# Depthwise convolution of 31 taps: four taps of a channel tile on ScalarE and GpSimd in place of TensorE

## The chip, the cores and the metric

One core of a Trainium2 chip runs the whole program in one launch. The metric is the time of that launch on the device, in microseconds, as the median of several runs; a profile of one execution stands beside it.

## The reference

Two transformer blocks run one after the other on 512 latent tokens (width 1024), the first with 256 context tokens beside them. The first block has a conformer convolution, a feed-forward with a convolution of width 3, a window attention and a second such feed-forward; the second block has an attention, a recurrent mixer, a memory attention and a third feed-forward. All is fp32. The change touches the conformer convolution alone, which runs near the start, for the latent and the context tokens:

```python
def dwconv(x, w, b):
    k = w.shape[0]                      # 31
    pad = (k - 1) // 2
    y = lax.conv_general_dilated(x, w[:, None, :], window_strides=(1,), padding=[(pad, pad)],
                                 dimension_numbers=('NWC', 'WIO', 'NWC'), feature_group_count=x.shape[-1])
    return y + b

def conformer_conv(h, w_pw1, b_pw1, w_dw, b_dw, ln_g, ln_b, w_pw2, b_pw2):
    u = h @ w_pw1 + b_pw1               # 1024 -> 2048
    a, g = jnp.split(u, 2, axis=-1)
    v = a * jax.nn.sigmoid(g)
    v = dwconv(v, w_dw, b_dw)           # each channel by itself, 31 taps along the tokens
    v = jax.nn.silu(layernorm(v, ln_g, ln_b))
    return v @ w_pw2 + b_pw2
```

## The kernel before

Channels lie on the 128 partitions and tokens along the free dimension, so a width of 1024 is eight channel tiles (`KT`). Every matrix product of the two blocks is made of three matmuls over high and low parts (`mm3`, L155 to L165): a weight half of 128x1024 is cast to its high part on ScalarE (`wh`, L143), and VectorE subtracts that from the raw weight for the low part (`wl`, L144). The raw weights come by DMA on SP's queue.

The convolution's stage is a loop over `j`, the channel tiles. `pw1(j)` does the first matrix product for tile `j` into five PSUM banks taken in turn; ScalarE takes the sigmoid of the gate, and VectorE writes the gated product `v` (L542 for the context, L543 for the latent tokens) into one of two buffers `vb`. A tile of `v` is 832 columns: 512 latent and 256 context tokens with zeros for the padding between and around them, so that one instruction over 798 columns (`AW`) does one tap for both.

The 31 taps of a tile are shared out by `NPE`. The first 4 x `NPE[j]` are TensorE's. For these `pw1(j)` writes `v` to DRAM (`vd`) and reads it back four times, with each group of 32 channels laid out four times at shifts of 0 to 3 columns (`S`). `diagonals(j)` makes 32x32 diagonal blocks of the tap weights on VectorE (`dg`, L571), and `dwconv(j)` multiplies (L583): one matmul does four taps of 32 channels, four of them make 128 channels, `NPE[j]` of those follow each other into one PSUM tile, for the latent and for the context part. The remaining taps are `taps(j)`: VectorE multiplies a shifted `v` by one weight per channel and adds it to `accp` (L560). The first of them is a product alone, on ScalarE for tiles 0 and 1 (L562), and from tile 2 on it adds `negc`, an offset taken from tile 0 (L564). `accp` and `prod` have two buffers each. At the end of `dwconv(j)` VectorE evicts: PSUM plus bias plus `accp` into `y` (L585).

The code issues for each `j`: `pw1(j)`, `taps(j)`, one or two pieces of a modulation product (`ada_pe`, L370, with raw weights of its own), the sums of squares of tile `j` - 2 (`sums`, L605 to L613, ScalarE writes the square into `prod`), and then `diagonals(j - 1)` and `dwconv(j - 1)`. The last tile is split into its latent and context part so that the layer norm can start early. The order on each engine is not that of the code: a planner orders the instructions by priority and by its own costs before the launch, puts in the semaphores, and from then on each engine's queue is fixed and in order. A buffer is taken again when its last reader is done.

GpSimd does nothing in this stage but a few fills of constants at its start.

Of the kernel before, what the change touches and what calls it, by code (L numbers as in the profile page):

```python
# [11 lines left out]
AF = mybir.ActivationFunctionType  # L12
ALU = mybir.AluOpType
# [4 lines left out]
KT = D // 128  # L18
SEQ = 512
CTX = 256  # L20
TOK = SEQ + CTX
# [30 lines left out]
def build(tc, ins, out, stop=None, dbg=None):  # L52
    ctx = ExitStack()
    with ctx:
        _build(ctx, tc, ins, out, stop, dbg)


def _build(ctx, tc, ins, out, stop, dbg):
    nc = tc.nc
    pe, act, dve, pool, sp = nc.tensor, nc.scalar, nc.vector, nc.gpsimd, nc.sync  # L60
# [32 lines left out]
    def ps(cols=512, tag="mm", parts=128):  # L93
        n = cur.turn.get(tag, 0)
        cur.turn[tag] = n + 1
        p, bufs = cur.tags[tag][n % len(cur.tags[tag])]
        return p.tile([parts, cols], F32, tag=tag, bufs=bufs, name=tag)

    def wk(cols, tag, bufs=1, dt=F32, parts=128, first=False):

        p, bufs = cur.sm, cur.bufs.get(tag, bufs)
        if cur.st and tag in ("cv", "u"):
            n = cur.turn.get(tag, 0)
            cur.turn[tag] = n + 1
            p, bufs = (cur.st, 2) if first or n % bufs < 2 else (p, bufs - 2)
        return p.tile([parts, cols], dt, tag=tag, bufs=bufs, name=tag)
# [15 lines left out]
    def V(name, i=0, n=1):  # L122
        o, c = _VOFF[name]
        assert i + n <= c
        return vec[:, o + i : o + i + n]
# [304 lines left out]
    SW = C0 + CTX + 16  # L430
    AW = C0 + CTX
    FILL = (0, 2, 2, 2, 2, 1, 1, 1, 1)
    NPE = (4, 4, 4, 4, 4, 4, 4, 5)
    ORD = (8, 'x', 9, 10, 'q', 11)
    LAT, CT = slice(0, SEQ), slice(SEQ, TOK)
    cur.raw, cur.w = 3, 3
# [4 lines left out]
    with sub("a_x", "xp"), sub("a_w", "wp"), sub("a_s", "sm"):  # L441
# [11 lines left out]
        R = wk(TOK, "sg")  # L453
        S = None
        for k in range(KT):
            q = wk(TOK, "prod", 2)
            for t, s in zip(h[k], (LAT, CT)):
                act.activation(out=q[:, s], in_=t, func=AF.Square)
            if S is None:
                S = q  # L460
            else:
                S2 = wk(AW, "accp", 2)[:, 0:TOK]
                dve.tensor_tensor(out=S2, in0=S, in1=q, op=ALU.add)
                S = S2
# [44 lines left out]
        dwt = wk(512, "dwt")  # L509
# [41 lines left out]

        def taps(j):

            acc = wk(AW, "accp", 2)
            v = vb[j % 2]
            for a, b in ((0, AW),) if j < KT - 1 else ((0, SEQ), (C0, AW)):
                for t in range(4 * NPE[j], 31):
                    w, x = dwt[:, 256 + 32 * j + t : 257 + 32 * j + t], v[:, t + a : t + b]
                    if t > 4 * NPE[j]:
                        dve.scalar_tensor_tensor(out=acc[:, a:b], in0=x, scalar=w, in1=acc[:, a:b], op0=ALU.mult, op1=ALU.add)  # L560
                    elif j < 2:
                        act.activation(out=acc[:, a:b], in_=x, func=AF.Copy, scale=w)  # L562
                    else:
                        dve.scalar_tensor_tensor(out=acc[:, a:b], in0=x, scalar=w, in1=negc[:, a:b], op0=ALU.mult, op1=ALU.add)  # L564
            parts[j] = acc

        def diagonals(j):

            n = NPE[j]
            dg = wk(640, "dg", 1)[:, 0 : n * 128]  # L570
# [5 lines left out]
        def dwconv(j, dg, which=(0, 1)):  # L576
            n, S, acc = NPE[j], shifts[j], parts[j]
            pieces = [(ps((512, 256)[q]), (0, C0)[q], (512, 256)[q], (LAT, CT)[q]) for q in which]
            for m in range(n):
                for p, o, w, _ in pieces:  # L580
                    for g in range(4):
                        c = 32 * (n * g + m)
                        pe.matmul(p[32 * g : 32 * g + 32], dg[:, c : c + 32], S[g][:, 4 * m + o : 4 * m + o + w], start=m == 0, stop=m == n - 1, tile_position=(0, 32 * g))  # L583
            for p, o, w, s in pieces:
                dve.scalar_tensor_tensor(out=y[j][:, s], in0=p, scalar=V("b_dw", j), in1=acc[:, o : o + w], op0=ALU.add, op1=ALU.add)  # L585
            if j == 0:
                offset()
            elif j == 1:
                add_offset(y[1])
# [14 lines left out]

        def sums(j, which=(0, 1), sq=None):  # L605

            sq = sq or wk(TOK, "prod", 2)
            s = slice((LAT, CT)[which[0]].start, (LAT, CT)[which[-1]].stop)
            act.activation(out=sq[:, s], in_=y[j][:, s], func=AF.Square)
            for i in which:  # L610
                s = (LAT, CT)[i]
                for q, x in ((2 * i, y[j][:, s]), (2 * i + 1, sq[:, s])):
                    pe.matmul(SS[32 * q : 32 * q + 32, 0 : x.shape[1]], onec, x, start=j == 0, stop=j == KT - 1, tile_position=(0, 32 * q))  # L613
            return sq

        fill = list(range(KT, 3 * KT))
        for j in range(KT + 1):
            if j < KT:
                pw1(j)
                taps(j)  # L620
            if j == KT - 1:
                ws2 = pw2_weights((0, 1, 2))
            for _ in range(FILL[j]):
                ada_pe(fill.pop(0), scp)
            if j > 1:
                sums(j - 2)
            if 0 < j < KT:
                dwconv(j - 1, diagonals(j - 1))
# [30 lines left out]
        sq = None  # L659
        for i in range(2):  # L660
            dwconv(KT - 1, last, (i,))
            sq = sums(KT - 1, (i,), sq)
            if i == 0:
                load_table(AF.Sqrt, sq)
                norm_stats(0)
# [8 lines left out]

        def normed(k, i):
            s = (LAT, CT)[i]
            t, e = wk(AW, "accp", 2)[:, s], wk(TOK, "prod", 2)[:, s]
            dve.tensor_tensor(out=t, in0=y[k][:, s], in1=mean[:, s], op=ALU.subtract)
            dve.tensor_tensor(out=t, in0=t, in1=R[:, s], op=ALU.mult)
            if i == 0 and k == 0:  # L680
                act.activation(out=X[k][0][:, s], in_=t, func=AF.Silu, scale=V("ln_g", k), bias=V("ln_b", k))
            act.activation(out=e, in_=t, func=AF.Silu, scale=V("ln_g", k), bias=V("ln_b", k))
            if i or k:
                act.activation(out=X[k][0][:, s], in_=e, func=AF.Copy)
            dve.tensor_tensor(out=X[k][1][:, s], in0=e, in1=X[k][0][:, s], op=ALU.subtract)
# [6 lines left out]
        for i, s in enumerate((LAT, CT)):  # L692
            for k in range(KT):
                if i == 0 and k == 4:
                    norm_stats(1)
                normed(k, i)
                if i == 0 or k < 4:
                    for w, t in zip(ws2, tiles):
                        mm3([(t[i], s)], w, X[k], k == 0, k == KT - 1, k * 128)
# [9 lines left out]
        for m in range(3, KT):  # L709
            t = (ps(512), ps(256))  # L710
# [159 lines left out]
    for x in ORD:  # L870
        if x == "x":
            normed()
        elif x == "q":
            queries(0)
        else:
            key_value(x)
# [402 lines left out]
    with sub("e_x", "xp"), sub("e_w", "wp"), sub("e_t", "sm"):  # L1279
# [7 lines left out]
        t = wk(4, "t4", 2)  # L1287
# [433 lines left out]
```

## Time and profile before

| | us |
|---|---|
| three timed runs | 2319.4, 2327.75, 2331.1 |
| their median | 2327.75 |
| the profiled execution | 2321.32 |
| its span, first to last instruction | 2319.5 |

The page gives the busy time of each engine as a share of the span: TensorE 2230.0 us (96%), VectorE 1625.6 (70%), ScalarE 934.7 (40%), GpSimd 157.6 (7%). Busy TensorE is no proof of a full TensorE, since the ends of matmuls are modelled; what ended a wait, and which chain of work ended last, says more. The convolution's stage is the stretch from about 60 to 290 us.

### The profile page before, as it was taken

How to read it: one execution, taken by the hardware profiler on the slowest of the kernel's cores; microseconds unless marked ns; L12 is line 12 of the kernel's file. 1: busy time of each engine (PE TensorE's matmuls, PEld its weight loads, DVE VectorE, ACT ScalarE, POOL GpSimd, SP SyncE). 2: the span in 40 equal slices, each digit the busy share in tenths (PEclk: the TensorE clock that was granted, in tenths of full speed). 3: DMA queues.
4: the chain of work that ended last, by engine and by line, in shares of the span. 5: the costliest groups of instructions: out<-in, count | busy, mean ns of one | idle time of the engine just before them, and what ended most of it. 6: DMA issues, size and time to landing. Idle time of an engine off the chain costs nothing.

```text
span 2319.5 us, 36251 instructions
## 1 busy us (share of the span) xinstructions
PE 2230.0 (96%) x14910; PEld 1834.4 (79%) x14910; DVE 1625.6 (70%) x2625; ACT 934.7 (40%) x1626; POOL 157.6 (7%) x210
## 2 busy tenths in 40 slices
PE   4999999999999999999999999999999879999999
PEld 2767588888888888766689999997777777788887
DVE  4788759877677768776587777677564456866675
ACT  4222544223323324566663443335654323433332
POOL 0000000000000000155400000000331100000000
PEclk7999999999999999999999999999999899999999
DMA  8464414232233212330032222313111003222221
GB/s 321 139 230 163 168 61 167 100 121 108 91 120 117 93 54 74 114 105 28 10 146 92 96 105 73 110 37 108 46 40 35 26 21 118 75 107 91 100 82 55
DMA packets 50817, 228.82 MB, mean 99 GB/s; under 512 B 6331, under 2 KB 10972, under 8 KB 32220
## 3 DMA queue, kind: packets, MB, share of 16 engines
q1 hardware_dynamic: 50652, 226.51, 27.9%
q8 instruction: 117, 1.92, 0.3%
q14 instruction: 48, 0.39, 0.1%
HBM read 213.51 MB, written 6.68 MB: 95 GB/s over the span
## 4 chain that ended last, share of the span: by engine, by line
PE 89%; DVE 5%; ACT 3%; DMA 2%; issue 1%; POOL 0%; SPq 0%; DVEq 0%; ACTq 0%; POOLq 0%
PE mm L161 24%; PE mm L163 24%; PE mm L165 24%; PE mm L583 2%; PE po L916 2%; PE aux L912 1%; PE mm L790 1%; PE aux L370 1%; DMA raw<-in_ada 1%; PE sc L894 1%; PE rw L1447 1%; PE rw L1442 1%; PE sc L895 1%; PE rw L1437 1%; PE wo L161 0%
## 5 line engine op out<-in xcount | busy, mean ns | idle before, releaser
L161 PE MATMUL mm<-xh,wh 128*128 128x512 f32 (+2 forms) x2336 | 660.8, 339 | 15.6 <-ACT xh L486 5.1
L163 PE MATMUL mm<-xl,wh 128*128 128x512 f32 (+2 forms) x2336 | 663.3, 337 | 4.0 <-DVE xl L219 2.1
L165 PE MATMUL mm<-xh,wl 128*128 128x512 f32 (+2 forms) x2336 | 662.1, 337 | 0.7 <-DVE wl L144 0.7
L143 ACT ACTIVATE wh<-raw 128x1024 fp32r<-128x1024 f32 x263 | 274.8, 1057 | 538.4 <-PE mm L163 482.7
L161 PEld LDWEIGHTS mm<-xh,wh 128*128 128x128 f32 x2336 | 410.1, 191 | 70.8 <-ACT xh L486 7.2
L163 PEld LDWEIGHTS mm<-xl,wh 128*128 128x128 f32 x2336 | 411.1, 190 | 55.5 <-DVE xl L488 3.3
L165 PEld LDWEIGHTS mm<-xh,wl 128*128 128x128 f32 x2336 | 411.0, 190 | 48.7 <-DVE wl L144 1.3
L144 DVE TENSOR_TENSOR wl<-raw,wh 128x1024 fp32r<-128x1024 f32 x263 | 324.6, 1243 | 45.3 <-ACT wh L143 39.8
L161 PE MATMUL mm<-gh,wh 128*128 128x512 f32 (+1 forms) x704 | 255.4, 371 | 2.1 <-ACT gh L288 2.0
L163 PE MATMUL mm<-gl,wh 128*128 128x512 f32 (+1 forms) x704 | 254.5, 367 | 0.0
L165 PE MATMUL mm<-gh,wl 128*128 128x512 f32 x704 | 253.9, 366 | 0.0
L161 PEld LDWEIGHTS mm<-gh,wh 128*128 128x128 f32 x704 | 132.2, 189 | 28.1 <-ACT gh L288 2.4
L249 DVE TENSOR_TENSOR u<-mm,R 128x256 f32<-128x256 f32 x88 | 37.4, 425 | 161.8 <-PE mm L165 160.0
L165 PEld LDWEIGHTS mm<-gh,wl 128*128 128x128 f32 x704 | 131.2, 189 | 23.4
L163 PEld LDWEIGHTS mm<-gl,wh 128*128 128x128 f32 x704 | 131.2, 189 | 22.2
L310 DVE SCALAR_TENSOR_TENSOR hl<-mm,mod,hl 128x512 f32<-128x512 f32 x176 | 130.9, 745 | 20.3 <-PE mm L165 19.7
L288 ACT ACTIVATE gh<-cv 128x512 fp32r<-128x512 f32 (+1 forms) x66 | 46.5, 704 | 231.3 <-DVE cv L286 223.2
L271 DVE SCALAR_TENSOR_TENSOR cv<-u,vec,cv 128x512 f32<-128x512 f32 (+1 forms) x132 | 110.2, 835 | 9.6 <-ACT cv L262 8.6
L560 DVE SCALAR_TENSOR_TENSOR accp<-v,dwt,accp 128x798 f32<-128x798 f32 (+2 forms) x118 | 113.8, 974 | 2.6
L272 DVE SCALAR_TENSOR_TENSOR cv<-u,vec,cv 128x512 f32<-128x512 f32 (+1 forms) x132 | 110.5, 838 | 3.1
L284 ACT ACTIVATE cv<-cv 128x512 f32<-128x512 f32 (+1 forms) x66 | 46.4, 703 | 114.2 <-DVE cv L272 114.1
L397 DVE SCALAR_TENSOR_TENSOR ac<-ra,sc,ac 128x512 f32<-128x512 f32 x112 | 81.7, 742 | 2.0 <-DMA ra<-in_ada 1.8
(474 smaller groups left out, 2992.0 us busy)
## 6 DMA issues: line engine op xcount, KB each, us to landing
raw<-in_up SPq DMA_DIRECT2D x63, 1024.0 KB, 4.8
raw<-in_dn SPq DMA_DIRECT2D x33, 1024.0 KB, 4.8
raw<-in_ada SPq DMA_DIRECT2D x24, 1024.0 KB, 5.7
ra<-in_ada SPq DMA_DIRECT2D x48, 512.0 KB, 3.3
raw<-in_pw SPq DMA_DIRECT2D x12, 1024.0 KB, 6.0
S<-vd SPq DMA_DIRECT2D x28, 407.0 KB, 5.6
raw<-in_w_in SPq DMA_DIRECT2D x17, 512.0 KB, 3.3
raw<-in_qkv SPq DMA_DIRECT2D x6, 1024.0 KB, 5.5
```

The source lines that it names most:

```text
L143: act.activation(out=hi, in_=part, func=AF.Copy)
L144: dve.tensor_tensor(out=lo, in0=part, in1=hi, op=ALU.subtract)
L161: pe.matmul(p, whi[:, c], xhi[:, s], start=first, stop=False)
L163: pe.matmul(p, whi[:, c], xlo[:, s], start=False, stop=False)
L165: pe.matmul(p, wlo[:, c], xhi[:, s], start=False, stop=last)
L271: dve.scalar_tensor_tensor(out=cv[:, 0:CW], in0=u[:, 0:CW], scalar=wv[0], in1=cv[:, 0:CW], op0=ALU.mult, op1=ALU.add)
L272: dve.scalar_tensor_tensor(out=cv[:, 0:CW], in0=u[:, 2 : 2 + CW], scalar=wv[2], in1=cv[:, 0:CW], op0=ALU.mult, op1=ALU.add)
L284: act.activation(out=ca[:, 0:CW], in_=ca[:, 0:CW], func=AF.Silu)
L288: act.activation(out=gh[:, 0:CW], in_=cb[:, 0:CW], func=AF.Copy)
L310: dve.scalar_tensor_tensor(out=hs, in0=p, scalar=g2[i][:, m : m + 1], in1=hs, op0=ALU.mult, op1=ALU.add)
L397: dve.scalar_tensor_tensor(out=a, in0=t[:, q, :], scalar=sc2[:, k, n : n + 1], in1=a, op0=ALU.mult, op1=ALU.add)
L560: dve.scalar_tensor_tensor(out=acc[:, a:b], in0=x, scalar=w, in1=acc[:, a:b], op0=ALU.mult, op1=ALU.add)
```

## The change

`NPE` falls from 4 to 3 for tiles 0 to 6, so TensorE does the first 12 taps there in place of 16. `taps(j)` runs on VectorE over taps 12 to 26 in place of 16 to 30. Taps 27 to 30 of these tiles are new code: for each, ScalarE multiplies the shifted `v` by the weight into a `prod` buffer, and GpSimd adds that to `accp`. The last tile keeps its 20 taps on TensorE and 11 on VectorE. `prod` becomes 798 columns wide in place of 768, and its other users take the first 768. Nothing else changes; the shift copies `S` stay as wide as they were.

```diff
-    NPE = (4, 4, 4, 4, 4, 4, 4, 5)
+    NPE = (3, 3, 3, 3, 3, 3, 3, 5)
...
-            q = wk(TOK, "prod", 2)
+            q = wk(AW, "prod", 2)[:, 0:TOK]
...
         def taps(j):
             acc = wk(AW, "accp", 2)
             v = vb[j % 2]
             for a, b in ((0, AW),) if j < KT - 1 else ((0, SEQ), (C0, AW)):
-                for t in range(4 * NPE[j], 31):
+                for t in range(4 * NPE[j], 31 if j == KT - 1 else 27):
...
+            if j < KT - 1:
+                for t in range(27, 31):
+                    x = wk(AW, "prod", 2)
+                    act.activation(out=x, in_=v[:, t : t + AW], func=AF.Copy, scale=dwt[:, 256 + 32 * j + t : 257 + 32 * j + t])
+                    pool.tensor_tensor(out=acc, in0=acc, in1=x, op=ALU.add)
             parts[j] = acc
...
-            sq = sq or wk(TOK, "prod", 2)
+            sq = sq or wk(AW, "prod", 2)[:, 0:TOK]
...
-            t, e = wk(AW, "accp", 2)[:, s], wk(TOK, "prod", 2)[:, s]
+            t, e = wk(AW, "accp", 2)[:, s], wk(AW, "prod", 2)[:, 0:TOK][:, s]
```

## Rows read from the trace of the kernel before

**Rows 1.** The page: two engines in 40 slices; the chain that ended last.

```profile
PE   4999999999999999999999999999999879999999
...
POOL 0000000000000000155400000000331100000000
...
PE 89%; DVE 5%; ACT 3%; DMA 2%; issue 1%; POOL 0%; SPq 0%; DVEq 0%; ACTq 0%; POOLq 0%
```

**Rows 2.** Windows: stretch, length; busy us of PE, PEld, DVE, ACT, POOL; PEclk.

```profile
88.60:113.05 24.45, 24.45 (x178) 17.67 (x172) 23.23 (x28) 5.72 (x8) 0.00 (x0) 1.00 0.38 131
113.05:138.05 25.00, 25.00 (x188) 17.72 (x184) 22.74 (x26) 4.02 (x5) 0.00 (x0) 1.00 0.60 210
138.05:163.07 25.02, 25.02 (x189) 17.70 (x184) 20.66 (x23) 3.90 (x5) 0.00 (x0) 1.00 0.60 211
163.07:187.64 24.57, 24.57 (x185) 17.47 (x180) 19.72 (x24) 12.12 (x21) 0.00 (x0) 1.00 0.61 214
187.64:211.80 24.16, 24.16 (x181) 17.48 (x176) 20.96 (x23) 5.21 (x7) 0.00 (x0) 1.00 0.50 174
211.80:229.01 17.21, 17.21 (x123) 11.73 (x116) 16.62 (x18) 1.65 (x3) 0.00 (x0) 1.00 0.56 184
```

**Rows 3.** VectorE's groups, 88.6 to 229.01: busy us, mean ns, idle before, releasers.

```profile
L560 DVE SCALAR_TENSOR_TENSOR accp<-v,dwt,accp 128x798 f32<-128x798 f32 x86 | 89.8, 1048 | 2.1
L144 DVE TENSOR_TENSOR wl<-raw,wh 128x1024 fp32r<-128x1024 f32 x11 | 13.4, 1221 | 5.1 <-ACT wh L143 5.1
...
L571 DVE TENSOR_TENSOR dg<-eye,dwt 128x512 f32<-128x512 f32 x6 | 4.1, 680 | 0.0
L543 DVE SCALAR_TENSOR_TENSOR v<-mm,vec,sg 128x512 f32<-128x512 f32 x5 | 3.8, 750 | 8.9 <-PE mm L165 6.3 <-issue 2.7
```

**Rows 4.** The chain in order of time, the matmuls of one tile: start, us.

```profile
87.61 5.30 PE mm L583 x64
```

**Rows 5.** ScalarE's groups, 70 to 250: the first tap of tiles 0 and 1.

```profile
L562 ACT ACTIVATE accp<-v,dwt 128x798 f32<-128x798 f32 x2 | 1.9, 956 | 0.0
```

**Rows 6.** GpSimd's groups over the whole span, by form.

```profile
L1414 POOL TENSOR_TENSOR NM<-NM,t 128x256 f32<-128x256 f32 x6 | 4.4, 728 | 46.0 <-DVE NM L1412 46.0
...
L1254 POOL TENSOR_TENSOR t<-t 128x512 f32<-128x512 f32 x3 | 3.8, 1281 | 16.4 <-DVE AR L1252 16.4
```

**Rows 7.** VectorE in order of time: start, us, instruction, idle before.

```profile
1683.75 1.75 DVE L1301 SCALAR_TENSOR_TENSOR r<-cv,vec,u 128x512 f32<-128x512 f32 x1
```

**Rows 8.** GpSimd in the same stretch.

```profile
1683.66 1.30 POOL L1228 TENSOR_TENSOR t<-t 128x512 f32<-128x512 f32 x1 [2.44 <-DVE t L1227]
```

**Rows 9.** VectorE in order of time, 1704.5 to 1710.

```profile
1707.59 1.10 DVE L1261 SCALAR_TENSOR_TENSOR t<-t,vec,r 128x512 f32<-128x512 f32 x1
1708.61 0.47 DVE L1130 CUSTOM_DVE_ANT_0 s<-sc,bias,vec 128x256 f32<-128x256 f32 x1
...
1709.62 0.75 DVE L1301 SCALAR_TENSOR_TENSOR r<-cv,vec,u 128x512 f32<-128x512 f32 x1 [0.53 <-POOL cv L1300]
```

**Rows 10.** VectorE in order of time, 955 to 959.

```profile
956.15 2.10 DVE L144 TENSOR_TENSOR wl<-raw,wh 128x1024 fp32r<-128x1024 f32 x1
```

**Rows 11.** GpSimd in that stretch.

```profile
955.43 1.74 POOL L803 TENSOR_TENSOR cv<-cv,rope 128x512 f32<-128x512 f32 x1 [19.22 <-DMA cv<-u]
```

**Rows 12.** GpSimd in order of time, 1704.5 to 1710.

```profile
1708.10 1.49 POOL L1300 TENSOR_TENSOR cv<-u 128x512 f32<-128x512 f32 x1
```

**Rows 13.** VectorE in order of time at the last channel tile.

```profile
229.01 0.75 DVE L543 SCALAR_TENSOR_TENSOR v<-mm,vec,sg 128x512 f32<-128x512 f32 x1 [0.17 <-PE mm L165]
...
253.66 0.75 DVE L585 SCALAR_TENSOR_TENSOR y<-mm,vec,accp 128x512 f32<-128x512 f32 x1 [5.09 <-PE mm L583]
```

**Rows 14.** The chain in order of time at the last channel tile.

```profile
235.93 9.74 DMA raw<-in_ada
```

**Rows 15.** VectorE in order of time at tile 0's eviction.

```profile
91.86 3.92 DVE L560 SCALAR_TENSOR_TENSOR accp<-v,dwt,accp 128x798 f32<-128x798 f32 x4
...
98.23 1.14 DVE L585 SCALAR_TENSOR_TENSOR y<-mm,vec,accp 128x512 f32<-128x512 f32 x2
```

## The prediction

> **What bounds the kernel now.** I read the page first: the 40 slices and the chain that ended last [rows 1]. TensorE has a 9 in nearly every slice and 89% of the chain, and GpSimd has nothing at all in the slices of the convolution (slices 2 to 5, some 60 to 260 us). So a product that leaves TensorE leaves the engine that sets the time, and it goes to one that is idle there. That is the case for the change, and the rest asks who else is nearly full.
>
> Second, the windows of the convolution, cut where TensorE starts the work behind one channel tile [rows 2]. A tile takes 24.2 to 25.0 us. [...] VectorE is busy for 23.2, 22.7, 20.7, 19.7, 21.0 of these, and for 16.6 of the 17.2 us of the last stretch: 123.9 us of 140.4 together, 16.5 us idle. ScalarE is busy for 4 to 12 us of a tile. So TensorE is first, and VectorE stands 12% behind it: whatever costs VectorE more than some 2.7 us a tile turns the order round.
>
> Third, what VectorE waits for there: the groups by line [rows 3]. Of its idle time 8.9 us is at the gated product `v` (L543), for TensorE, and 5.1 us at the low part of a weight (L144), for ScalarE. The first sort goes when VectorE comes late; the second partly.
>
> **What is removed.** Each of tiles 0 to 6 loses one of four diagonal groups. The chain has the 64 matmuls of one tile (each product is two instructions) in 5.30 us [rows 4]; 16 of 64 are worth 1.3 us. Seven tiles make 9.1 us, and six of them, 7.8 us, lie in the stretch that the sum below uses. VectorE's `dg` (L571) falls from 512 to 384 columns: less than a quarter of its 680 ns [rows 3], I take 0.14 us a tile, over six tiles 0.8 us. The taps left to VectorE are 15 a tile as before (12 to 26 in place of 16 to 30). The shift copies and every DMA stay, so SP's queue is past nothing new.
>
> **What is added on ScalarE.** 28 products of 128x798. The like of it stands in the trace, 956 ns [rows 5]: 3.8 us a tile, into 12 us or more of idle. Two of a tile's four can run early, since `prod` has two buffers; the other two wait until GpSimd has read a buffer, and the weight casts (L143) and sigmoids stand behind them in ScalarE's queue. I price that at nothing: L144 already waits 5.1 us for casts [rows 3] and TensorE, which needs both, still never stands [rows 2]. What it costs if that slack is gone is among the rivals.
>
> **What is added on GpSimd.** 28 sums of 128x798, each reading two SBUF tiles. The trace has sums of 256 at 728 ns and of 512 columns at 1281 [rows 6]; by that slope 798 columns take 1.28 + 286 x 0.553/256 = 1.9 us, 7.6 us a tile. All four read and write `accp`, so they run behind the tile's last tap on VectorE, beside the taps of the next tile, and the eviction L585 on VectorE waits for the fourth.
>
> **What these sums do to VectorE.** This is the term that decides. Where GpSimd runs a tensor operation later in the kernel and VectorE one with two SBUF inputs, the one holds up the other. An L1301, the same kind of instruction as a tap, takes 1.75 us [rows 7] when it starts behind a GpSimd product of 1.30 us [rows 8]; it takes 0.75 alone [rows 9]. It lost 1.00 us, 77% of the GpSimd instruction. An L144, 1.22 us alone, takes 2.10 [rows 10], while the GpSimd product beside it goes from 1.28 to 1.74 [rows 6, 11]: VectorE lost 0.88, GpSimd 0.46. The mildest case is an L1261 that had started first: 1.10 in place of 0.75 [rows 9], and then GpSimd's L1300 takes 1.49 [rows 12]. An instruction that reads PSUM beside that L1300 shows no loss: L1130, 0.47 us [rows 9]. So it looks like turns at something that GpSimd shares with a second SBUF input. For a sum of 1.9 us the loss is 0.77 x 1.9 = 1.5 us. Below, the mildest case gives 0.35; above, VectorE waits for the whole sum, 1.9 less the 0.2 us by which its start overlaps, 1.7.
>
> Not every sum meets such an instruction. Right behind a tile's last tap stand L543 and L542 of the next tile (1.2 us, reading PSUM), which cover most of one sum. Taps, L144, `dg` and the small additions are about nine tenths of the rest. I take 3.3 of four sums: 5.0 us a tile, 1.25 us a sum, near to the upper rows because VectorE has its instructions back to back here.
>
> [...]
>
> **The sum.** VectorE's work from 88.60 to 229.01 us becomes 123.9 + 6 x 5.0 - 0.8 = 153.1 us. Of its 16.5 us of waits I keep 4, since casts and loads still tie it. That is 157 us where TensorE would need 140.4 - 7.8 = 132.6, so VectorE sets the pace, and TensorE waits for low parts and for `v`. The stretch grows by about 17 us. What follows carries it on: `v` of tile 7 leaves VectorE at 229.01 with 0.17 us of wait [rows 13], right behind the last tap of tile 6, and the late modulation loads, which need a buffer that VectorE's L144 frees just behind it, are in the chain with a DMA of 9.74 us [rows 14]. Tile 6's own sums cost 5 us more on VectorE, but the eviction at 253.66 had waited 5.09 us for TensorE [rows 13], which covers them. If that cover were gone, they would add up to 5. Behind the convolution TensorE is the bound again and gives nothing back.
>
> The profiled execution took 2321.32 us (span 2319.5). With 17 us it is 2338. The three timed runs have a median of 2327.75, 6.4 above the profiled one; on that median I forecast 2344.
>
> **The rivals.** A measurement of this kernel can tell some 0.5%, 11.6 us, from no change. In general the stretch moves by 24 x (loss per sum) - 13.3 us, down to the -7.8 that TensorE sets.
>
> *TensorE stays the bound (not slower).* If a sum costs VectorE under 0.2 us, the waits at `v` shrink and each tile ends 1.3 us earlier: -9, 2319 on the median. From 0.55 us a sum this mechanism no longer holds the time below that of before. For it: 16.5 us of idle, a GpSimd with nothing else to do, the mildest row. Against it: the 1.75 and 2.10 us. 12%.
>
> *Half the price.* VectorE gets in first as often as not, or the order puts the sums beside PSUM readers: 0.7 us a sum, +3.5, 2331. For it: L1261. Against it: taps stand back to back. 22%.
>
> *The sums come late.* VectorE and ScalarE wait for GpSimd on top of the turns. Tile 0's last taps end by 95.8 and its eviction starts at 98.23 [rows 15]: 2.5 us, where four sums in turns with taps need 4 x 1.9 + 3 x 0.9 = 10.3; for tile 1 the gap is some 5 us. If the order is kept, VectorE stands 8 + 5 us there, with the taps of the next tiles behind it and the offset matmul on TensorE: +30, 2358. For it: both queues are in order, and products 3 and 4 hold up casts on ScalarE. Against it: the planner sees the sums and can put the eviction later, and a standing VectorE pays no turns. 16%.
>
> **How the numbers follow.** My forecast, sums in turns with taps, has 50%. Its own bounds are 1.0 and 1.7 us a sum: +11 to +30 with the tail, 2339 to 2358. The range has to reach to the half price and to most of the late sums: 2321 to 2361. Slower by over 0.5% is the late sums and most of the forecast: 58%. Within 0.5%: TensorE's case mostly, the half price, the low end of the forecast: 37%. Faster by more takes TensorE's case with a gain outside these rows: 5%.
>
> **What would show it.** In the profile of the changed kernel: 48 matmuls of L583 a tile in about 3.9 us; GpSimd with some 28 sums in 70 to 250 us that take over 1.9 us where taps run beside them; the mean of L560 from 1.05 to about 1.35 us (its 86 instructions would share 26 us or so); TensorE no longer busy throughout 88 to 229 us but idle for some 3 us a tile, ended by VectorE; the wait at L543 gone; the eviction of tile 7 near 270 us. Wrong if L560 stays at 1.05 (no turns), if TensorE stays full (the first rival), or if the idle time of VectorE grows with GpSimd as its releaser (late sums).

## The result and the profile after

The changed kernel takes 2350.72 us (median of 4 runs, 2346.67 to 2354.54) beside 2323.57 for the kernel before in the same session: a ratio of 1.0125, interval 1.0098 to 1.0152. It is slower, and by more than the 17 us that were forecast: the interval is 23 to 35 us, and the profiled execution is 2346.67 us (span 2344.8) in place of 2321.32, 25.3 us. The 2350.72 lies in the range given, 2321 to 2361. That it lies so near to the 2344 is in part luck: the forecast stood on a median of 2327.75 for the kernel before, and a fourth run brought that to 2323.57. By the difference it is 27 us where 17 were forecast.

The page of the changed kernel, two engines in 40 slices, and its chain that ended last by engine:

```profile
PE   4998799999999999999999999999999979999999
...
POOL 0134200000000000154400000000241100000000
...
PE 81%; DVE 11%; ACT 3%; DMA 2%; issue 2%; POOL 1%; SPq 0%; DVEq 0%; ACTq 0%; POOLq 0%
```

GpSimd now works in slices 2 to 5. TensorE has an 8 and a 7 there, and in the chain it gave up 8 points to VectorE, 5% to 11%, and others [rows 1]. The order of the two engines is turned round, as forecast. The windows with the columns of [rows 2], cut at the start of `v` (L543) of tiles 1 to 7:

```profile
88.71:115.24 26.53, 25.24 (x169) 17.26 (x173) 25.98 (x23) 8.83 (x11) 10.20 (x4) 1.00 0.40 141
115.24:143.64 28.40, 28.40 (x211) 18.55 (x202) 28.19 (x28) 7.18 (x9) 9.10 (x4) 1.00 0.51 187
143.64:172.06 28.42, 24.58 (x156) 17.78 (x155) 28.14 (x25) 8.12 (x10) 9.70 (x4) 0.94 0.53 198
172.06:201.50 29.44, 22.96 (x127) 17.12 (x129) 27.56 (x28) 15.04 (x24) 10.93 (x5) 0.83 0.41 149
201.50:226.60 25.10, 25.10 (x188) 17.28 (x191) 23.99 (x22) 8.99 (x11) 7.53 (x4) 1.00 0.50 171
226.60:248.60 22.00, 21.90 (x152) 16.20 (x148) 21.65 (x20) 7.26 (x9) 9.72 (x4) 1.00 0.39 141
```

The windows of [rows 2] were cut up to 1.6 us later. The whole stretch of the kernel before, cut at `v` too:

```profile
87.60:229.01 141.41, 141.41 (x1028) 100.13 (x1028) 124.92 (x139) 33.10 (x49) 0.00 (x0) 1.00 0.54 188
```

So it is 159.89 us in place of 141.41, 18.5 longer, and begins 1.1 us later. VectorE (third busy number) is busy for 155.50 of it: 4.4 us idle, where before it was 16.5. TensorE looks full in three windows and is not in the two with a granted clock of 0.94 and 0.83: there it stood 3.31 and 6.48 us for a square from ScalarE. VectorE was busy for 28.1 and 27.6 us of these two windows, so the two waits set little; the run own_squares below, which hardly has them, bears this out.

VectorE's groups from 88.7 to 248.6 us, the columns and lines of [rows 3] (L561 is the tap, L577 is `dg`):

```profile
L561 DVE SCALAR_TENSOR_TENSOR accp<-v,dwt,accp 128x798 f32<-128x798 f32 x85 | 111.6, 1318 | 1.8
L144 DVE TENSOR_TENSOR wl<-raw,wh 128x1024 fp32r<-128x1024 f32 x11 | 15.6, 1421 | 1.0 <-ACT wh L143 1.0
L565 DVE SCALAR_TENSOR_TENSOR accp<-v,dwt,negc 128x798 f32<-128x798 f32 x5 | 10.6, 2110 | 0.1
L577 DVE TENSOR_TENSOR dg<-eye,dwt 128x384 f32<-128x384 f32 x6 | 6.7, 1121 | 0.0
L543 DVE SCALAR_TENSOR_TENSOR v<-mm,vec,sg 128x512 f32<-128x512 f32 x7 | 5.2, 747 | 1.7 <-PE mm L165 1.7
```

The tap's mean went from 1048 to 1318 ns, `wl` from 1221 to 1421, and `dg` got longer although it has fewer columns. `v`, which reads PSUM, kept its 747. The longer means make 23.0 + 2.2 + 5.3 + 3.5 = 34.0 us (L565 had 1048 before; 0.54 is taken for `dg`), 1.42 us for each of 24 sums. Neighbouring records overlap a little, so by the windows it is less: 155.5 - 124.9 + 0.8 = 31.4, 1.31 us a sum.

Where the time goes can be seen one instruction at a time. VectorE behind tile 1:

```profile
118.74 1.04 DVE L561 SCALAR_TENSOR_TENSOR accp<-v,dwt,accp 128x798 f32<-128x798 f32 x1
...
120.03 2.68 DVE L565 SCALAR_TENSOR_TENSOR accp<-v,dwt,negc 128x798 f32<-128x798 f32 x1
122.75 2.58 DVE L561 SCALAR_TENSOR_TENSOR accp<-v,dwt,accp 128x798 f32<-128x798 f32 x1
125.25 2.27 DVE L577 TENSOR_TENSOR dg<-eye,dwt 128x384 f32<-128x384 f32 x1
127.44 3.78 DVE L561 SCALAR_TENSOR_TENSOR accp<-v,dwt,accp 128x798 f32<-128x798 f32 x2
131.13 1.22 DVE L144 TENSOR_TENSOR wl<-raw,wh 128x1024 fp32r<-128x1024 f32 x1
```

and GpSimd in that stretch, and its 28 sums as a group:

```profile
119.95 9.33 POOL L570 TENSOR_TENSOR accp<-accp,prod 128x798 f32<-128x798 f32 x4 [11.82 <-DVE accp L561]
```

```profile
L570 POOL TENSOR_TENSOR accp<-accp,prod 128x798 f32<-128x798 f32 x28 | 66.9, 2389 | 196.7 <-DVE accp L561 194.9 <-ACT prod L569 0.3
```

While the four sums run, 119.95 to 129.28, VectorE starts one instruction per sum and each takes 2.3 to 2.7 us. Once they are done it takes 1.22 for `wl` again. From 88.7 to 248.6 us VectorE is never idle with GpSimd as its releaser: its waits there are 1.7 us for TensorE (L543) and 1.0 for ScalarE (L144).

### The profile page after: what moved, and what is told of

Its sections match the earlier page's. It is cut to its first block, busy times and chain, and to the rows that moved or that the text cites. A ratio compares the mean times of both kernels' runs of the same rounds, so it can differ in the third digit from the quotient of the medians.

```text
span 2344.8 us, 36121 instructions
## 1 busy us (share of the span) xinstructions
PE 2229.4 (95%) x14798; PEld 1830.6 (78%) x14798; DVE 1658.6 (71%) x2625; ACT 962.8 (41%) x1656; POOL 225.4 (10%) x238
## 4 chain that ended last, share of the span: by engine, by line
PE 81%; DVE 11%; ACT 3%; DMA 2%; issue 2%; POOL 1%; SPq 0%; DVEq 0%; ACTq 0%; POOLq 0%
PE mm L161 22%; PE mm L163 22%; PE mm L165 22%; DVE accp L561 4%; PE po L922 1%; PE aux L918 1%; DVE wl L144 1%; DMA raw<-in_pw 1%; PE sc L900 1%; PE rw L1453 1%; PE mm L796 1%; PE rw L1448 1%; PE sc L901 1%; PE rw L1443 1%; DMA raw<-in_ada 1%
## 5 line engine op out<-in xcount | busy, mean ns | idle before, releaser
L144 DVE TENSOR_TENSOR wl<-raw,wh 128x1024 fp32r<-128x1024 f32 x263 | 324.2, 1242 | 41.3 <-ACT wh L143 36.7
L561 DVE SCALAR_TENSOR_TENSOR accp<-v,dwt,accp 128x798 f32<-128x798 f32 (+2 forms) x118 | 140.9, 1206 | 2.2
L570 POOL TENSOR_TENSOR accp<-accp,prod 128x798 f32<-128x798 f32 x28 | 66.9, 2389 | 196.7 <-DVE accp L561 194.9
```

Source lines behind the costliest of these rows:

```text
L144: dve.tensor_tensor(out=lo, in0=part, in1=hi, op=ALU.subtract)
L570: pool.tensor_tensor(out=acc, in0=acc, in1=x, op=ALU.add)
```

## The experiments

Two places to compare are the start of `v` of tile 7, 229.01 us before [rows 13] and 248.59 after, and the stretch from `v` of tile 1 to it, 141.4 us before. The stretch is the cleaner of the two: `v` of tile 0 already starts anywhere from 69.91 us (no_sums_own) to 75.21 (sums_alone), 73.04 in the kernel before, although no instruction ahead of it differs. "At the end" is the shift of VectorE's last stages against the kernel before, in the one profiled execution of each.

| run | median, before beside it | ratio, interval | stretch | `v` of tile 7 | at the end |
|---|---|---|---|---|---|
| changed kernel | 2350.72, 2323.57 | 1.0125 (1.0098 to 1.0152) | 159.9 | 248.6 | +25.3 |
| sums_alone | 2342.79, 2322.79 | 1.0096 (1.0079 to 1.0113) | 163.2 | 258.2 | +24.4 |
| no_sums | 2323.36, 2322.79 | 0.9997 (0.9980 to 1.0013) | 139.9 | 225.8 | +4.1 |
| no_sums_own | 2319.76, 2326.20 | 0.9978 (0.9963 to 0.9993) | 133.7 | 218.2 | -1.8 |
| own_squares | 2343.75, 2326.20 | 1.0080 (1.0054 to 1.0107) | 159.6 | 247.4 | +23.1 |
| two_sums | 2327.09, 2326.20 | 1.0004 (0.9987 to 1.0021) | 140.7 | 227.9 | +5.1 |
| dve_taps | 2328.79, 2322.79 | 1.0034 (1.0020 to 1.0048) | 150.1 | 237.5 | +8.7 |
| dve_three | 2328.14, 2326.20 | 1.0016 (0.9997 to 1.0034) | 137.9 | 223.1 | +5.3 |
| before_own | 2326.30, 2323.97 | 1.0009 (0.9990 to 1.0028) | 141.7 | 230.1 | +2.7 |
| dve_three_own | 2329.14, 2323.97 | 1.0023 (1.0005 to 1.0041) | 137.9 | 225.8 | +12.5 |

**Half of the change: no sums.** From the changed kernel, the line of the sums goes.

```diff
                 for t in range(27, 31):
                     x = wk(AW, "prod", 2)
                     act.activation(out=x, in_=v[:, t : t + AW], func=AF.Copy, scale=dwt[...])
-                    pool.tensor_tensor(out=acc, in0=acc, in1=x, op=ALU.add)
```

> The changed kernel without its 28 sums on GpSimd (taps 27 to 30 of tiles 0 to 6 are left out of the output); the products on ScalarE stay. Turns (each sum costs VectorE some 1.4 us): with the sums gone TensorE is the bound again and 9 us shorter, so about 9 us below the kernel before (ratio 0.996), L561 at 1.05 us in place of 1.28, v of tile 7 near 221 us. Rival, the change costs by itself what it costs (fewer matmuls in a new planned order, 28 products in ScalarE's queue): still 10 to 25 us above the kernel before. The rival in which ScalarE's queue stands behind buffers that GpSimd frees late gives the time of the first here, since nothing reads the buffers.

A miss in size. The extra time is gone, so the sums are what costs; but the 9 us that TensorE should have gained did not come: the ratio is 0.9997. Forty-eight matmuls do take 3.9 to 4.0 us a tile. But the squares of a finished tile go into `prod`, behind ScalarE's products in the same two buffers, and come late. TensorE's sum-of-squares matmuls (L618) in this run, in order of time, are torn apart:

```profile
184.70 0.59 PE L618 MATMUL ss<-y,onec 128*32 128x512 f32 x1
185.13 0.59 PE L618 MATMUL ss<-y,onec 128*32 128x512 f32 x1
193.25 0.62 PE L618 MATMUL ss<-prod,onec 128*32 128x512 f32 x1
193.25 0.40 PE L618 MATMUL ss<-y,onec 128*32 128x256 f32 x1
```

**The squares in a buffer of their own, without and with the sums.** `y[7]` is free until the last tile, so the squares of tiles 0 to 5 can go there, first in no_sums, then in the whole changed kernel.

```diff
-            sq = sq or wk(AW, "prod", 2)[:, 0:TOK]
+            sq = sq or (y[KT - 1] if j < KT - 2 else wk(AW, "prod", 2)[:, 0:TOK])
```

> No sums on GpSimd (taps 27 to 30 of tiles 0 to 6 are left out of the output), and the squares of tiles 0 to 5 (L614) go into the y buffer of tile 7, free until its eviction, in place of a prod buffer. Without sums the products alone left the kernel before where it was, 0.9997, and in that trace the four sum-of-squares matmuls of a tile no longer run together: three of them stand inside the next product, 1 us more a tile. Theory: TensorE's 9.1 us was given back there, because the squares had to queue for prod behind the products; with buffers of their own the four run together again: 5 to 8 us below the kernel before (ratio 0.9965 to 0.998), v of tile 7 near 220 us in place of 225.8. Rival: the gain is hidden behind loads at the last tile (the modulation weights' DMA), then v of tile 7 comes earlier and the time stays at 1.000.

Met. The eight matmuls of a tile are together again in no_sums_own:

```profile
202.07 1.03 PE L618 MATMUL ss<-y,onec 128*32 128x512 f32 x8
```

In the stretch, from the start of one matmul to the start of the next, TensorE spends 28.5 us on the diagonals in no_sums and 25.6 in no_sums_own, and 5.1 and 2.2 us on the sums of squares: 5.7 of the 6.2 us by which the stretch is shorter. (The other 1.4 us between 225.80 and 218.16 stood already at `v` of tile 0.) So the gain forecast for TensorE was real, and sharing `prod` took it. Even so, sums that cost nothing would have brought only 0.2% here.

> The changed kernel with the squares of tiles 0 to 5 in the y buffer of tile 7. In the changed kernel TensorE stood 9.8 us for squares that queued behind GpSimd's sums. Theory (VectorE sets the pace, its 28 turns of 1.4 us): these waits lie beside a full VectorE, so the time stays within 4 us of the changed kernel (ratio 1.010 to 1.014 against the kernel before). Rival (the loss is in waits for prod buffers on ScalarE and TensorE): 8 us or more faster than the changed kernel, ratio 1.008 or below.

By its number this is the rival's case: 1.0080 is the edge that was set for it, 10 us below the changed kernel by the ratios, though with four runs of each the intervals overlap (1.0098 to 1.0107). The traces speak for the theory as far as the convolution goes. TensorE's waits for squares at L619 fall from 9.8 us to 1.0, and VectorE is as full as before: in the stretch from `v` of tile 1 to that of tile 7 it is busy for 157.0 of 159.6 us. The stretch hardly moves. What moves is the tail behind it, told below; by 320 us the two kernels are 4.1 us apart. The rest of the 10 us is in no trace.

**The sums by themselves.** The kernel before, with 28 sums on GpSimd that read `v` and write a free tile, for which nobody waits.

```diff
+            if j < KT - 1:
+                for t in range(27, 31):
+                    pool.tensor_tensor(out=y[KT - 1], in0=y[KT - 1], in1=v[:, t : t + TOK], op=ALU.add)
```

> The kernel before with its 16 taps on TensorE, no products on ScalarE, and beside it 28 sums on GpSimd of 128x768 (the shifted v into a buffer that is overwritten later, so the output is the reference's). Nobody waits for these sums. Turns: VectorE loses 28 x 1.3 = 36 us, of which the idle time takes some 13: 17 to 24 us above the kernel before, L560 at 1.25 us or more. Late sums or a blocked ScalarE queue (the rival): no change, within 3 us of the kernel before, since nothing waits for GpSimd. Lost by the new order of the matmuls: no change either.

Met. Nothing that VectorE does has changed and nobody waits for a sum, yet the taps of this run take 1408 ns in place of 1048:

```profile
L560 DVE SCALAR_TENSOR_TENSOR accp<-v,dwt,accp 128x798 f32<-128x798 f32 x85 | 119.4, 1408 | 2.1
```

That excludes the late sums as the main cause: the same slowness comes without any dependence.

**The price by itself.** A program of its own, which computes nothing of the reference: 16 instructions on VectorE, 8 on GpSimd, each alone and then both at once, in tiles that have nothing in common.

```python
two:    dve.scalar_tensor_tensor(out=x, in0=y, scalar=one, in1=x, op0=ALU.mult, op1=ALU.add)      # L33
psum:   dve.scalar_tensor_tensor(out=x[:, 0:512], in0=ps, scalar=one, in1=x[:, 0:512], ...)       # L36
single: dve.tensor_scalar(out=x, in0=y, scalar1=one, scalar2=None, op0=ALU.mult)                  # L39
sums:   pool.tensor_tensor(out=gx, in0=gx, in1=gy, op=ALU.add)                                    # L42
product: pool.tensor_scalar(out=gx, in0=gy, scalar1=one, scalar2=None, op0=ALU.mult)              # L45
fill:   pool.memset(gx, 0.0)                                                                      # L48
```

> A program of its own that computes nothing of the reference: stretches of 16 equal instructions on VectorE (or ScalarE) and 8 on GpSimd, each alone and together, over 798 fp32 columns. Turns at a second SBUF input: a multiply-add of two SBUF tensors goes from 1.05 us to about twice that beside GpSimd's sums, while the same with one input in PSUM (512 columns, 0.75 us) and ScalarE's product (0.95 us) stay; sums go from 1.9 us to 2.5 or more. Rival, the sums take SBUF bandwidth from everything: ScalarE's product and the PSUM form slow down as well. Open: whether a VectorE product with one SBUF tensor, a GpSimd product with one input, and a GpSimd fill take turns too; if only two inputs on both sides matter, they stay at their times alone.

VectorE in order of time (start, us for all 16):

```profile
4.95 17.34 DVE L33 SCALAR_TENSOR_TENSOR x<-y,one,x 128x798 f32<-128x798 f32 x16 [0.73 <-ACT x L30]
39.43 29.20 DVE L33 SCALAR_TENSOR_TENSOR x<-y,one,x 128x798 f32<-128x798 f32 x16 [17.14 <-ACT y L30]
69.31 12.55 DVE L36 SCALAR_TENSOR_TENSOR x<-ps,one,x 128x512 f32<-128x512 f32 x16 [0.68 <-ACT x L30]
82.51 12.54 DVE L36 SCALAR_TENSOR_TENSOR x<-ps,one,x 128x512 f32<-128x512 f32 x16 [0.66 <-ACT x L30]
99.11 10.74 DVE L39 TENSOR_SCALAR x<-y,one 128x798 f32<-128x798 f32 x16 [4.05 <-ACT y L30]
110.59 22.59 DVE L39 TENSOR_SCALAR x<-y,one 128x798 f32<-128x798 f32 x16 [0.75 <-ACT y L30]
153.92 21.70 DVE L33 SCALAR_TENSOR_TENSOR x<-y,one,x 128x798 f32<-128x798 f32 x16 [20.74 <-ACT y L30]
184.21 17.34 DVE L33 SCALAR_TENSOR_TENSOR x<-y,one,x 128x798 f32<-128x798 f32 x16 [8.59 <-ACT y L30]
```

GpSimd in the same program, 8 of a kind:

```profile
23.28 15.47 POOL L42 TENSOR_TENSOR gx<-gx,gy 128x798 f32<-128x798 f32 x8 [22.84 <-ACT gy L30]
39.73 20.46 POOL L42 TENSOR_TENSOR gx<-gx,gy 128x798 f32<-128x798 f32 x8 [0.98 <-ACT gy L30]
82.90 15.52 POOL L42 TENSOR_TENSOR gx<-gx,gy 128x798 f32<-128x798 f32 x8 [22.71 <-ACT gy L30]
...
134.28 18.96 POOL L45 TENSOR_SCALAR gx<-gy,one 128x798 f32<-128x798 f32 x8 [6.24 <-issue]
154.24 21.90 POOL L45 TENSOR_SCALAR gx<-gy,one 128x798 f32<-128x798 f32 x8 [1.01 <-ACT gy L30]
```

As the theory of turns has it for taps; what it did not foresee, the instruction with one input, stands in the last section. Taps alone take 17.34 us and sums alone 15.47, 1.93 each. Together the taps take 29.20: 11.86 us more, 1.48 for each sum, and the sums take 2.56 each. With one operand in PSUM neither side loses anything (12.55 and 12.54; the sums 15.47 and 15.52), and neither does ScalarE's product (16 of them in 15.84 us alone and 15.85 beside the sums), so the rival in which the sums take bandwidth from everything is out. This fits turns at something that the two engines share on the SBUF side; what that is, the program does not show. Had VectorE stood for the whole of each sum, one would have cost it 1.93; 1.48 is 77% of that.

**Half of the sums.** Only taps 27 and 28 as product and sum (29 and 30 are left out of the output).

```diff
-                for t in range(27, 31):
+                for t in range(27, 29):
```

> The changed kernel with two products and two sums a tile in place of four (taps 29 and 30 of tiles 0 to 6 are left out of the output). Theory: VectorE loses 14 x 1.42 = 20 us, and its idle time of the kernel before (some 13 us) takes most of it; the stretch to v of tile 7 moves by 12 x 1.42 - 13.3 = +4 us, so 2 to 7 us above the kernel before, much less than half of the changed kernel's 27. Rival (each sum adds its price to the time, with no slack first): half of it, 13 us.

Lower than forecast: 0.9 us above the kernel before by the medians (interval -3 to +5), where 2 to 7 were forecast, and `v` of tile 7 is at 227.94, 1.1 us before [rows 13]. Against no_sums the first twelve sums of the stretch add 0.7 us to it (139.9 to 140.7), and twelve more add 19.3 (to 159.9). VectorE's idle time pays for the first ones: it is busy for 123.3 of 139.9 us in no_sums and for 137.1 of 140.7 here. (This run also has half the products in `prod`, so the 0.7 is no clean price.) A cost in proportion to the sums would have been +9 in the stretch and +13 in all.

**The same taps on VectorE.** All 19 taps from 12 to 30 on VectorE, no products, no sums; then the same for tiles 3 to 5 only, with and without the squares in `y[7]`; and the squares in `y[7]` in the kernel before.

```diff
-                for t in range(4 * NPE[j], 31 if j == KT - 1 else 27):
+                for t in range(4 * NPE[j], 31):
...
-            if j < KT - 1:
-                for t in range(27, 31):
-                    ...
```

> 12 taps on TensorE in tiles 0 to 6 as in the changed kernel, but the four taps go to VectorE itself as ordinary taps: 19 a tile, no products, no sums. Turns: a tap costs VectorE 1.06 us where a sum of GpSimd's costs it 1.4, so this is 28 x 0.35 = 10 us faster than the changed kernel and still 12 to 18 us above the kernel before, with VectorE busy throughout. Rival in which GpSimd's part is cheap and the loss is in waits on ScalarE: at 28 x 1.06 = 30 us on VectorE this is no faster than the changed kernel, or slower.

The direction held and the size was better than expected: +0.3% where 12 to 18 us were forecast, and by the ratios (1.0125 and 1.0034) some 21 us less than the changed kernel. In the stretch the two are 9.9 us apart, the 10 that were forecast; by 320 us it is 15.9, and the rest is in no trace. VectorE's taps in this run:

```profile
L561 DVE SCALAR_TENSOR_TENSOR accp<-v,dwt,accp 128x798 f32<-128x798 f32 x112 | 111.2, 1046 | 0.1
```

They take 111.2 us of VectorE from 88.6 to 250 us, all 112 of them; in the changed kernel 85 taps took 111.6. Four taps a tile handed to GpSimd had cost VectorE more than doing them: it is busy for 155.5 us of the stretch in the changed kernel and for 141.8 here, where it is not full (150.1).

```diff
-    NPE = (3, 3, 3, 3, 3, 3, 3, 5)
+    NPE = (4, 4, 4, 3, 3, 3, 4, 5)
```

> A group of four taps goes from TensorE to VectorE itself in tiles 3, 4 and 5 alone, where VectorE was idle for 3 to 5 us of a tile; no products, no sums. Theory: VectorE gets 4.2 us in each of these and just fits, TensorE is 1.3 us shorter in each: 0 to 4 us below the kernel before (ratio 0.998 to 1.000). Rival: the low parts of weights come late behind the longer chain of taps, and it is 2 to 5 us above.

A miss by its number, 1.0016, though the interval reaches to 0.9997. The stretch is 3.5 us shorter and the convolution ends 3.9 us earlier, so the late low parts of the rival are not seen; but from some 900 us on the gain goes, and the whole is 5.3 us late in the profiled execution.

```diff
-            sq = sq or wk(TOK, "prod", 2)
+            sq = sq or (y[KT - 1] if j < KT - 2 else wk(TOK, "prod", 2))
```

> The kernel before, with the squares of channel tiles 0 to 5 written into y[7] in place of prod and nothing else changed. If sharing prod costs only where ScalarE's products share it too (my theory), the kernel before, which has no products there, gains nothing: 0.998 to 1.001, v of tile 7 within 1 us of 229.0. Rival: the shared buffer costs the kernel before as well (its layer norm and sums use both buffers), and part of the 11.8 us between no_sums and no_sums_own was never the products': ratio 0.995 to 0.998, v of tile 7 near 224.

Met (1.1 us at `v` of tile 7, where 1 was allowed, and 0.2 us in the stretch): without products on ScalarE the shared buffer costs the kernel before nothing.

> VectorE has taps 12 to 30 of tiles 3 to 5 and TensorE keeps 16 taps in the others, without products or sums, and the squares of tiles 0 to 5 go into y[7]. TensorE has three groups fewer than before, 3.9 us at 1.3 us a group, and VectorE 12 taps more, 12.6 us, against 16.5 us of idle time. If the later stages' own order takes back what the convolution gains (as in dve_three, 3.9 us earlier there and 5.3 later at the end), the ratio is 0.999 to 1.003. If the squares' waits had a part in that, it is 0.996 to 0.998 and v of tile 7 near 221; this would be a version faster than both.

The first of the two cases: no gain. The stretch is that of dve_three, 137.9 us, so the squares' waits had no part in it. That it ends later than dve_three is not shown: the profiled execution, 2333.86 us, is the longest of its twelve, and the medians are within each other's intervals. No kernel that computes the whole came out faster than the one before.

## Why the prediction was right, and which terms were too small

**TensorE first, VectorE close behind it.** Right. No_sums leaves TensorE the bound and costs nothing, and in two_sums the two engines are level (137.7 and 137.1 us busy of 140.7); with 28 sums VectorE is busy for 155.5 of 159.9 us and TensorE waits for others.

**What is removed.** Right in size: 48 matmuls in about 4 us, and in no_sums_own the stretch from tile 1 to tile 7 is 133.7 us in place of 141.4, 7.7 of the 7.8 forecast. That it can be had without a price was wrong, see below, but with VectorE as the bound nothing hung on it.

**The loss per sum.** Forecast 1.25 us, measured 1.31 by the windows and 1.42 by the groups. The rate was right: 77% of the sum, from the one pair in [rows 7, 8], is what the probe shows, 1.48 of 1.93. Too small was the share of sums that meet such an instruction, 3.3 of four: 1.31 to 1.42 of 1.48 is 3.5 to 3.8. In the stretch shown, no reader of PSUM lies beside the four sums at all. Over 24 sums it is 31.4 in place of 30.0 us.

**The waits kept.** 4 forecast, 4.4 measured. So the stretch grew by 16.7 + 1.4 + 0.4 = 18.5 us, and that is all of it. Of the signs named, the tap's mean (1.35 forecast, 1.32 measured) and the vanishing wait at L543 held (1.7 us are left of 8.9). The eviction of tile 7 was forecast near 270 and began at 274.05. TensorE idle for 3 us in each tile did not show: 10.3 of its 11.7 us lie in two of the six windows, and in the others its records, whose ends are modelled, fill the time.

**The term that was missing: the price of nothing on ScalarE's `prod`, and with it the cover at the tail.** Tile 6's sums were to be hidden by the 5.09 us for which the last eviction waited [rows 13]. VectorE's share of them was: that wait fell to 0.86. But the squares come late. ScalarE, VectorE and TensorE of the changed kernel behind `v` of tile 7:

```profile
262.53 0.84 ACT L615 ACTIVATE prod<-y 128x768 f32<-128x768 f32 x1 [1.06 <-POOL accp L570]
264.81 0.84 ACT L615 ACTIVATE prod<-y 128x768 f32<-128x768 f32 x1 [1.43 <-POOL accp L570]
...
265.64 0.81 DVE L577 TENSOR_TENSOR dg<-eye,dwt 128x640 f32<-128x640 f32 x1
...
274.05 0.75 DVE L591 SCALAR_TENSOR_TENSOR y<-mm,vec,accp 128x512 f32<-128x512 f32 x1 [0.86 <-PE mm L589]
...
266.56 6.08 PE L589 MATMUL mm<-S,dg 128*32 128x512 f32 x35 [3.12 <-ACT prod L615]
```

VectorE and TensorE of own_squares at the same place:

```profile
264.85 0.81 DVE L577 TENSOR_TENSOR dg<-eye,dwt 128x640 f32<-128x640 f32 x1
...
265.76 6.38 PE L589 MATMUL mm<-S,dg 128*32 128x512 f32 x40 [2.58 <-issue]
```

The four sums hold both `prod` buffers, so the squares of tiles 4 and 5 are made at 262.53 and 264.81; in own_squares they are at 213.8 and 240.1. The view puts TensorE's wait of 3.12 us in front of the last tile's diagonals to such a square. That can't be: the square ends 0.9 us before these matmuls start, and own_squares, with no square in front of them, has the wait too. In both kernels they start 0.1 us behind the end of VectorE's `dg`, their other operand. The price is paid behind that. The sums of squares of tiles 4 and 5, sixteen matmuls, now stand among and behind the last diagonals. From the first of these to the last eviction it takes 7.49 us (6.45 in own_squares), and to the next load of modulation weights, which starts at 275.76, it takes 9.20 (7.30 in own_squares).

Earlier in the stage such waits lay beside a full VectorE. ScalarE's and TensorE's waits (60 or 70 to 290 us; total, times, longest):

```profile
ACT prod L569 <- POOL accp L570: 60.1, 18, 13.1
```

```profile
PE ss L619 <- ACT prod L615: 9.8, 2, 6.5
```

From `v` of tile 7 to the stages after the convolution the shift grew from 19.6 to 22.8 us. In own_squares, where those squares don't need `prod`, it goes from 18.4 to 18.7: the 3 us are the buffer's. The slack that the prediction cited, 5.1 us of `wl` waiting for casts [rows 3], was that of the wrong user; the casts were in time, the squares were not.

**What follows carries it on.** Mostly: the shift is 22.8 us from 320 to about 900 us. Then it drifts to 25.3. All kernels here drift behind 900 us, between 4.8 us less (sums_alone) and 10.7 more (dve_three_own), although no instruction there differs. The traces show two reasons. The first is the granted clock. In sums_alone, before_own and dve_taps VectorE, ScalarE and GpSimd have their instructions from 330 us on in the very order of the kernel before, and still the shift changes by -4.8, +1.7 and +1.8 us. The same instructions in the kernel before and in before_own, with the columns of [rows 2]:

```profile
1912.00:1927.00 15.00, 13.61 (x40) 9.03 (x41) 6.25 (x11) 1.96 (x5) 0.00 (x0) 0.66 0.00 0
```

```profile
1918.60:1933.60 15.00, 13.13 (x57) 9.14 (x58) 8.26 (x14) 2.05 (x5) 0.00 (x0) 1.00 0.00 0
```

The granted clock was 0.50 from 1916 to 1924 us in the one, 0.66 on the mean of the window, and 1.00 on the mean in the other. At 0.50 the 128x512 matmuls of the kernel before start 0.43 us apart, from 1927 us on, at 1.00, 0.23 us. In this stretch the shift of before_own went from 6.6 to 2.6 us. So a single execution carries some us that are not its kernel's: the 23 executions of the kernel before beside before_own lie between 2312.93 us, at a mean granted clock of 0.986, and 2333.06, at 0.978. What sets the granted clock the runs do not show. The second is the planner's order. No_sums_own, two_sums, dve_three and dve_three_own have one order behind 330 us, another than that of the kernel before, and all four lose 6.7 to 10.7 us behind 900 us. How much of this is the order itself, and how much the clock that goes with it, was not tried and stays open. It is as large as the gain that dve_three and no_sums_own have at the convolution.

So the 25.3 us are the 16.7 forecast, 1.4 for the share of sums, 0.4 of waits, 3.2 at the tail, and 1.1 ahead of the stretch and 2.5 of drift, which is no more than such scatter.

**The rivals.** TensorE as the bound fell with sums_alone. Half the price fell with the probe. The late sums were not there on VectorE, which the planner kept busy, but in small they were, by way of ScalarE, at the tail.

## What to carry to other kernels

Sums moved to an idle GpSimd were paid on VectorE where the instructions beside them read both operands, or the only one, from SBUF (16 of them went from 17.34 to 29.20 us, and from 10.74 to 22.59; all fp32): price a GpSimd sum of two tiles at some three quarters of its own time on VectorE (1.48 of 1.93 us), set that against VectorE's idle time in that stage, and compare it with doing the work on VectorE (here 1.3 to 1.4 us a sum beside 1.05 us a tap). Place such work beside instructions that read PSUM (12.54 us beside the sums, 12.55 alone), and keep it under the slack: half of these sums cost 0.7 us in the stretch, the other half 19. When a new producer takes turns in a shared buffer, ask who else writes that buffer and who waits for him, not only whether its engine has time. And where a view names the one that ended a wait, compare the times: here the named square had ended 0.9 us before.

## What the runs showed of the hardware

A VectorE instruction with a single SBUF input also lost to the sums: the 16 of L39 went from 10.74 to 22.59 us, 1.48 for each sum, as much as with two. Alone one of them takes 0.67 us, where a tap takes 1.08.

A GpSimd product with one input is no cheaper than a sum of two tiles: 2.37 us alone beside 1.93. But it costs VectorE only 0.55 us (21.70 - 17.34 over 8). A fill on GpSimd (0.81 us) costs VectorE nothing: 17.34 us with and without.
